# An earlier transpose of the dt rows, and another order in each MLP's last pair, in a one-core decoder step

## The chip, the cores and the metric

The kernel runs on one core of a Trainium2 chip. The time is that of the device for one execution, in microseconds (us). Below, PE is the tensor engine (matmul), DVE the vector engine, ACT the scalar engine, POOL the GpSimd engine and SP the engine that issues most transfers. "L367" is line 367 of the kernel before.

## What is computed

One step of a two-layer decoder trunk over 544 tokens: a prompt of 512, and 8 sequences of 4 tokens each with states of their own. The width is 1024, everything is float32.

```python
x = LN(alpha*x + ab_mixer(x));   x = LN(alpha*x + mlp(x))     # layer 0: mLSTM and GLA heads
x = LN(alpha*x + ssd_mixer(x));  x = LN(alpha*x + mlp(x))     # layer 1: Mamba-2 SSD
mlp(x) = square(relu(x @ w1)) @ w2                            # 1024 -> 4096 -> 1024
```

The SSD mixer needs, for each of 32 heads and each token, a step size and its running sums:

```python
dt = softplus(dtr + dt_bias);  a = dt * -exp(a_log)
cs = cumsum(a)                             # within a chunk
w  = exp(cs[t] - cs[s]) * dt[s]            # causal weights inside a chunk
wL = exp(cs[last] - cs) * dt               # weights of the chunk's final state
```

## The kernel before

Everything is held feature-major: features on the 128 partitions, tokens along the free dimension, in two halves of 272 tokens (`HALVES`). A float32 product is made of three products of a faster format: each operand is split into a high part (a cast on ACT, L166, L202, L286) and a low part (a subtraction on DVE, L167, L203, L287), and `hi*hi + hi*lo + lo*hi` accumulates in one PSUM bank. `dense` (L367) does this for one 128-column block of weights and one half of the tokens: 24 products for a depth of 1024. `WeightStream` loads the blocks in the order of use and splits them some blocks ahead.

**The order of the work.** PE's instructions run in the order in which the program writes them. The other engines' queues are ordered by the framework, which plans ahead of time by priority and by when it expects an instruction's inputs. Work beside the dense products is written as Python generators in lanes. `tick` is called ahead of every dense product; each lane counts its own ticks down and, at zero, writes its next piece. The counts stand in the table `W`. So a number in `W` says after how many dense products a piece stands in PE's queue.

**The SSD stage.** The first dense block of the stage gives `dt` before its softplus. `dt_rows` computes from it, on DVE and ACT, a tile `rows` with 32 partitions each of the running sums `cs`, of `dt` and of `dw` (the weights `wL`; its last operation is L1483). `rows` is one of two buffers that share the tag `E`. Then the generator `dt_cols` waits `W["dt"]` ticks from its launch, and transposes `rows` with five PE products into two PSUM banks, `rt` (L1489, L1490). Out of each bank it copies `cols` (L1493) and the negated `ncs` (L1494), and out of the second also `csp` (L1495). Then it says `dt` is ready. The generator `group(0)` in the lane "ssd" has waited for that: it transposes `Bf` into two banks (L1554, L1557), then in `scores` the tokens of the group into `xt` (L1578), multiplies `Cf` by `Bf` (`cb`, L1580), and goes on with `state` (L1614, L1617) and `outputs` (`yp`, L1639), with a fixed count of ticks between. Groups 1 to 3 follow in the same lane. All these small results take their PSUM bank in turn from four (`pm`). Meanwhile the convolution of the dense blocks runs on ACT (L1531, L1536) and DVE (`acc`, L1533; L1538, L1539).

**The MLP.** Hidden blocks 6 to 31 are made in pairs (`pair`) by a scheme of seven quarter products in place of eight. A quarter is 12 products (L563). The seven go into four banks `pa`, `pb`, `pc`, `pe`; three of the banks are used twice: the first sum of a bank is read, and then a second quarter accumulates onto it (`first=False`). The reads are `z = pa` (ACT, L623), `z += pb` (L626), `c22 = z + pc` (L629), `c22 += pe` (L632), then, after the second use, `c21 = z + pc` (L636), relu of `pa` (L612) and `c12 = z + pe` (L643). `act` makes of each result relu, square, high part and low part. `c21` and `pa` are the first half of the tokens, `c22` and `c12` the second. Pair 30 is the last; right after it the last part of the second matrix ("last", blocks 24 to 31) runs the first half of the tokens first, then the second. It reads block 30 at the seventh and block 31 at the eighth of its eight steps of depth.

Of the kernel before, what the change touches and what calls it, by code (L numbers as in the profile page):

```python
# [13 lines left out]
ALU = mybir.AluOpType  # L14
# [17 lines left out]
HEAD, TAIL = 5, 7  # L32
HEADM = 6

W = dict(dec=12, gates=30, gr=8, sc=16, lev=14, v=24, kd=10, out=38, ss=40, end=12, c0=20, u=13, s=16, ml=12, mr=40, dt=238, sg=72, sx=14, sq=26, so=48, l0=12, l1=12, v0=74, v1=55, f0=16, f1=18, f2=4, ls=20, vs=47)
LEVELS = (64, 32, 16, 8, 4, 2, 1)


# [189 lines left out]
def trunk_kernel(ctx, tc, a, stages=("ab", "mlp0", "ssd", "mlp1")):  # L228
    nc = tc.nc
    V, S, G, TE = nc.vector, nc.scalar, nc.gpsimd, nc.tensor  # L230
# [192 lines left out]
    def layernorm(hf, i, pool, out=None):  # L423
# [4 lines left out]
        which = norms_done[0] - hf  # L428
        yield W["l0" if not hf else "ls" if i == 2 else "l1"]
        mu = pm("mu")  # L430
# [8 lines left out]
        V.tensor_tensor(q[:, 0], q[:, 0], q[:, 1], ALU.add)  # L439
        yield W["v0" if not hf else "vs" if i == 2 else "v1"]  # L440
        var = pm("var")
# [34 lines left out]
    def last_layernorm(i, pool, out):  # L476
# [6 lines left out]
        def less(mu, k, f):  # L483
            V.scalar_tensor_tensor(x[:, k:k + 2], mu[:, None, :n].broadcast_to([P, 2, n]), f, x[:, k:k + 2], ALU.mult, ALU.add)
        yield W["f0"]
        mu = pm("mu")
# [9 lines left out]
        for k in range(h, KT - 1):  # L496
# [4 lines left out]
            V.tensor_tensor(q[:, 0], q[:, 0], q[:, k], ALU.add)  # L501
        yield W["f1"]
        mu, var, rp = pm("mu"), pm("var"), pm("rp")
        TE.matmul(mu[:, :n], ones, s, start=True, stop=False)
        yield W["f2"]
        TE.matmul(var[:, :n], ones, q[:, 0], start=True, stop=False)
# [50 lines left out]
    def quarter(w, b, ps, first):  # L557

        n = 0
        for k in range(4):  # L560
            for wt, bt in ((w[0], b[0]), (w[0], b[1]), (w[1], b[0])):
                tick()
                last[0] = TE.matmul(ps, wt[:, k], bt[:, k], start=first and n == 0, stop=n == 11, skip_group_check=not first).ins  # L563
                n += 1

    def mlp(l, phase_, outer, xp, out):
# [9 lines left out]
        bt = {}  # L576
# [31 lines left out]
        def act(m, hf, x, r=None):  # L608
            c0, c1 = HALVES[hf]
            h = place(m)  # L610
            r = hr() if r is None else r
            S.activation(r, x, AF.Relu)  # L612
            S.activation(r, r, AF.Square)
            split(h[0][:, c0:c1], h[1][:, c0:c1], r)

        def pair(m):
            w = ws.next()
            pa, pb, pc, pe = (bank()[:, :TH] for _ in range(4))
            hp = tc.high_priority
            z, c22, c21, c12 = (hr() for _ in range(4))  # L620
            quarter(w["a11"], bt["b11"], pa, True)
            with hp():
                S.copy(z, pa)  # L623
            quarter(w["s2"], bt["t2"], pb, True)
            with hp():
                V.tensor_tensor(z, z, pb, ALU.add)  # L626
            quarter(w["s3"], bt["t3"], pc, True)
            with hp():
                V.tensor_tensor(c22, z, pc, ALU.add)  # L629
            quarter(w["s1"], bt["t1"], pe, True)  # L630
            with hp():
                V.tensor_tensor(c22, c22, pe, ALU.add)  # L632
                act(m + 1, 1, c22, c22)
            quarter(w["a22"], bt["t4"], pc, False)
            with hp():
                V.tensor_tensor(c21, z, pc, ALU.add)  # L636
                act(m + 1, 0, c21, c21)
            quarter(w["a12"], bt["b21"], pa, False)
            with hp():
                act(m, 0, pa)  # L640
            quarter(w["s4"], bt["b22"], pe, False)
            with hp():
                V.tensor_tensor(c12, z, pe, ALU.add)  # L643
                act(m, 1, c12, c12)
# [10 lines left out]
        for kind, m, *r in MLP:  # L655
# [6 lines left out]
            if kind == "last":  # L662
                own.close()
                ws.lend(outer.enter_context(tc.tile_pool(name="hlx" + phase_, bufs=HLX, reuse_waits="tile")), phase_, HLX)
                end = None if out is None else lambda: last_layernorm(2 * l + 1, xp, out)
# [6 lines left out]
            for bs in blocks:  # L672
                w = ws.next()
# [720 lines left out]
    def ssd(pool, ypool, dram, right, ahead, consts):  # L1394
# [15 lines left out]
        cols = pool.tile([P, 5, 64], F32, name="scols", bufs=1)  # L1410
# [3 lines left out]
        dec = pool.tile([P, 32, 4], F32, name="dec", bufs=1)  # L1414
# [70 lines left out]
        def dt_cols():  # L1485
            yield W["dt"]
            p1, p2 = pm("rt"), pm("rt2")
            for b in range(4):
                TE.transpose(p1[:, b * 96:(b + 1) * 96], rows[:96, b * P:(b + 1) * P], ident[:96, :96])  # L1489
            TE.transpose(p2[:NS, :96], rows[:96, NP:], ident[:96, :96])  # L1490
            for o, b, q in ((slice(0, P), slice(0, 4), p1[:, :384].rearrange("p (b c) -> p b c", b=4)),
                            (slice(0, NS), slice(4, 5), p2[:NS, None, :96])):
                V.tensor_copy(cols[o, b], q[:, :, 32:])  # L1493
                V.tensor_scalar(ncs[o, b], q[:, :, :32], -1.0, None, ALU.mult)  # L1494
            V.tensor_copy(csp, p2[:NS, :32])  # L1495
            for r in (64, 96):
                S.activation(ecs[r:r + NS], ncs[:NS, 4], AF.Exp, scale=-1.0)
            ready.add("dt")
# [43 lines left out]
        Y, sqs, gates, tanh = [None] * 4, {}, {}, [None]  # L1542
# [327 lines left out]
    while n < len(stages):  # L1870
        st = stages[n]
        src = spill
        with ExitStack() as stk:
            if st == "ssd":
# [5 lines left out]
                with tc.tile_pool(name="ssd", bufs=1, reuse_waits="tile") as pool:  # L1880
# [4 lines left out]
                    with tc.manual_schedule(engines={mybir.EngineType.PE}):  # L1885
                        out = ssd(pool, ypool, dram, right, ahead, consts)
# [172 lines left out]
```

## Time and profile before

| what | us |
|---|---|
| median of three runs (1491.34 to 1493.38) | 1491.72 |
| the profiled execution | 1491.97 |
| its span, first to last instruction | 1490.2 |
| PE busy in it | 1468.6 |
| DVE busy | 1097.4 |
| ACT busy | 792.8 |

A row of the timeline gives the start, the duration, the engine, the line, the operation, what it writes and reads, and in brackets how long the engine stood idle ahead of it and what ended that. In the list of waits stand who waited for whom, and then the sum in us, the number of times and the longest. A product's row (0.29 us) is longer than its distance to the next one, since products overlap inside the engine.

### The profile page before, as it was taken

How to read it: one execution, taken by the hardware profiler on the slowest of the kernel's cores; microseconds unless marked ns; L12 is line 12 of the kernel's file. 1: busy time of each engine (PE TensorE's matmuls, PEld its weight loads, DVE VectorE, ACT ScalarE, POOL GpSimd, SP SyncE). 2: the span in 40 equal slices, each digit the busy share in tenths (PEclk: the TensorE clock that was granted, in tenths of full speed). 3: DMA queues.
4: the chain of work that ended last, by engine and by line, in shares of the span. 5: the costliest groups of instructions: out<-in, count | busy, mean ns of one | idle time of the engine just before them, and what ended most of it. 6: DMA issues, size and time to landing. Idle time of an engine off the chain costs nothing.

```text
span 1490.2 us, 29251 instructions
## 1 busy us (share of the span) xinstructions
PE 1468.6 (99%) x11637; PEld 1421.1 (95%) x11637; DVE 1097.4 (74%) x2073; ACT 792.8 (53%) x1746; POOL 190.8 (13%) x223
## 2 busy tenths in 40 slices
PE   9999999999999999999999999999999999999997
PEld 8999999999999999999888789899999999999996
DVE  4956576886776766678999988777588677676656
ACT  5645556473543453547886676555257355444333
POOL 0511231100000000010234342420010000000000
PEclk9999999999999999999999999999999999999999
DMA  6322325223332322525567866364222333233121
GB/s 225 97 71 58 117 60 167 73 69 98 100 92 94 97 88 71 156 98 161 136 185 228 255 182 209 100 211 138 72 75 71 99 97 99 86 100 100 57 86 60
DMA packets 94705, 172.90 MB, mean 116 GB/s; under 512 B 15960, under 2 KB 50392, under 8 KB 94312
## 3 DMA queue, kind: packets, MB, share of 16 engines
q1 hardware_dynamic: 61992, 140.86, 30.8%
q10 hardware_dynamic: 29216, 17.19, 4.5%
q0 software_dynamic: 3360, 12.98, 2.3%
q8 instruction: 91, 1.49, 0.4%
q14 instruction: 46, 0.38, 0.1%
HBM read 153.88 MB, written 17.13 MB: 115 GB/s over the span
## 4 chain that ended last, share of the span: by engine, by line
PE 43%; DVE 4%; DMA 2%; ACT 1%; issue 1%; POOL 0%; DVEq 0%; ACTq 0%; POOLq 0%
PE psd L367 30%; PE psd L563 9%; DMA E<-d_cs 2%; PE yp L1639 1%; PE it L1686 1%; DVE acc L1533 1%; DVE wlo L167 1%; PE sp L1617 1%; PE sps L1693 1%; DVE h0n L1699 0%; PE ip L1614 0%; ACT E L1599 0%; PE xt L1578 0%; POOL E L1593 0%; DVE xf L525 0%
## 5 line engine op out<-in xcount | busy, mean ns | idle before, releaser
L367 PE MATMUL psd<-xh,whi 128*128 128x272 f32 x1504 | 445.8, 296 | 0.1
L367 PE MATMUL psd<-xh,wlo 128*128 128x272 f32 x1504 | 439.9, 293 | 0.7 <-DVE wlo L167 0.7
L367 PE MATMUL psd<-xl,whi 128*128 128x272 f32 x1504 | 438.1, 291 | 1.8 <-DVE xl L451 1.3
L367 PE MATMUL psd<-hh,whi 128*128 128x272 f32 x1024 | 296.4, 289 | 0.7 <-ACT hh L286 0.7
L367 PE MATMUL psd<-hlo,whi 128*128 128x272 f32 x1024 | 295.9, 289 | 0.2
L367 PE MATMUL psd<-hh,wlo 128*128 128x272 f32 x1024 | 295.8, 289 | 0.0
L367 PEld LDWEIGHTS psd<-xl,whi 128*128 128x128 f32 x1504 | 284.1, 189 | 8.0 <-issue 4.2
L367 PEld LDWEIGHTS psd<-xh,whi 128*128 128x128 f32 x1504 | 283.5, 188 | 7.4 <-issue 5.1
L367 PEld LDWEIGHTS psd<-xh,wlo 128*128 128x128 f32 x1504 | 283.4, 188 | 4.9 <-issue 2.8
L167 DVE TENSOR_TENSOR wlo<-wraw,whi 128x1024 fp32r<-128x1024 f32 (+2 forms) x173 | 208.8, 1209 | 61.6 <-ACT whi L166 60.9
L166 ACT CAST whi<-wraw 128x1024 fp32r<-128x1024 f32 (+2 forms) x173 | 174.2, 1011 | 132.4 <-PE psd L367 114.8
L367 PEld LDWEIGHTS psd<-hh,whi 128*128 128x128 f32 x1024 | 193.1, 189 | 1.3 <-ACT hh L286 1.2
L367 PEld LDWEIGHTS psd<-hlo,whi 128*128 128x128 f32 x1024 | 193.0, 188 | 0.8 <-DVE hlo L287 0.6
L367 PEld LDWEIGHTS psd<-hh,wlo 128*128 128x128 f32 x1024 | 193.1, 189 | 0.1
L401 DVE TENSOR_TENSOR xf<-xf,psd 128x272 f32<-128x272 f32 x208 | 88.3, 434 | 75.9 <-PE psd L367 75.4
L563 PE MATMUL psd<-xh,wlo 128*128 128x272 f32 x416 | 120.1, 289 | 0.0
L563 PE MATMUL psd<-xh,whi 128*128 128x272 f32 x416 | 119.9, 288 | 0.0
L563 PE MATMUL psd<-xl,whi 128*128 128x272 f32 x416 | 119.8, 288 | 0.0
L202 ACT CAST whi<-wsum 128x1024 fp32r<-128x1024 f32 x52 | 54.3, 1044 | 111.0 <-PE psd L563 70.2
L202 ACT CAST whi<-wraw 128x1024 fp32r<-128x1024 f32 (+1 forms) x52 | 43.4, 834 | 95.3 <-PE psd L367 84.2
L203 DVE TENSOR_TENSOR wlo<-wsum,whi 128x1024 fp32r<-128x1024 f32 x52 | 63.7, 1224 | 23.2 <-ACT whi L202 23.2
L563 PEld LDWEIGHTS psd<-xl,whi 128*128 128x128 f32 x416 | 78.5, 189 | 0.0
(474 smaller groups left out, 2778.2 us busy)
## 6 DMA issues: line engine op xcount, KB each, us to landing
wraw<-mlp_w SPq DMA_DIRECT2D x80, 512.0 KB, 3.6
wraw<-ssd_in SPq DMA_DIRECT2D x40, 512.0 KB, 4.0
wraw<-mlp_w SPq DMA_DIRECT2D x64, 256.0 KB, 3.1
wraw<-ab_in SPq DMA_DIRECT2D x24, 512.0 KB, 3.6
h<-h SPq DMA_DIRECT2D x32, 256.0 KB, 4.9
h0n<-h0n SPq DMA_DIRECT2D x16, 512.0 KB, 5.7
E<-d_cs ACTq DMA_DIRECT2D x16, 512.0 KB, 4.5
s_h<-h0n POOLq DMA_DIRECT2D x16, 512.0 KB, 4.1
```

Of the source, the lines that this page charges most:

```text
L166: nc.scalar.copy(hi[:, r], w[:, r])
L167: nc.vector.tensor_tensor(lo[:, r], w[:, r], hi[:, r].bitcast(F32), ALU.subtract)
L202: self.cut[0] = nc.scalar.copy(hi, x).ins
L203: self.cut[1] = nc.vector.tensor_tensor(lo, x, hi.bitcast(F32), ALU.subtract).ins
L367: last[0] = TE.matmul(ps[:, :TH], wt[:, k, :], rt, start=i == 0, stop=i == n - 1).ins
L401: V.tensor_tensor(x, x, ps, ALU.add)
L563: last[0] = TE.matmul(ps, wt[:, k], bt[:, k], start=first and n == 0, stop=n == 11, skip_group_check=not first).ins
L1533: V.scalar_tensor_tensor(acc[:, :n], ci[:, w:w + n], cw[:, m, w:w + 1], acc[:, :n], ALU.mult, ALU.add)
L1617: TE.matmul(sp, Bt[:, b], xw, start=True, stop=True)
L1639: TE.matmul(ypv[64 * e:64 * e + 64, j], z[:, 64 * r:64 * r + 64], E[:, r], start=True, stop=True)
L1686: TE.matmul(it[64 + NS * k:64 + NS * k + NS], Cm[:, NS * (q + k):NS * (q + k) + NS], h0[k], start=q == 0, stop=q == NB - 2)
L1693: TE.matmul(sp[:, 256 * j:256 * j + 256], Xs[:, m * P:(m + 1) * P], Bm.rearrange("p k n -> p (k n)"), start=True, stop=True)
```

## The change

`W["dt"]` goes from 238 to 224 ticks. The two copies of `cols` go from DVE to ACT. In pair 30 of each MLP the two quarters that end the first half of the tokens come ahead of s1; the other pairs stay as they are.

```diff
-W = dict(..., dt=238, ...)
+W = dict(..., dt=224, ...)
...
-            quarter(w["s1"], bt["t1"], pe, True)
-            with hp():
-                V.tensor_tensor(c22, c22, pe, ALU.add)
-                act(m + 1, 1, c22, c22)
-            quarter(w["a22"], bt["t4"], pc, False)
-            with hp():
-                V.tensor_tensor(c21, z, pc, ALU.add)
-                act(m + 1, 0, c21, c21)
-            quarter(w["a12"], bt["b21"], pa, False)
-            with hp():
-                act(m, 0, pa)
+
+            def second():
+                quarter(w["s1"], bt["t1"], pe, True)
+                with hp():
+                    V.tensor_tensor(c22, c22, pe, ALU.add)
+                    act(m + 1, 1, c22, c22)
+
+            def first():
+                quarter(w["a22"], bt["t4"], pc, False)
+                with hp():
+                    V.tensor_tensor(c21, z, pc, ALU.add)
+                    act(m + 1, 0, c21, c21)
+                quarter(w["a12"], bt["b21"], pa, False)
+                with hp():
+                    act(m, 0, pa)
+
+            for half in (first, second) if m == 30 else (second, first):
+                half()
             quarter(w["s4"], bt["b22"], pe, False)
...
-                V.tensor_copy(cols[o, b], q[:, :, 32:])
+                S.copy(cols[o, b], q[:, :, 32:])
                 V.tensor_scalar(ncs[o, b], q[:, :, :32], -1.0, None, ALU.mult)
```

More of the change, by code (lines that the diff above doesn't have):

```diff
@@ L33 @@
 HEADM = 6
-W = dict(dec=12, gates=30, gr=8, sc=16, lev=14, v=24, kd=10, out=38, ss=40, end=12, c0=20, u=13, s=16, ml=12, mr=40, dt=238, sg=72, sx=14, sq=26, so=48, l0=12, l1=12, v0=74, v1=55, f0=16, f1=18, f2=4, ls=20, vs=47)
+W = dict(dec=12, gates=30, gr=8, sc=16, lev=14, v=24, kd=10, out=38, ss=40, end=12, c0=20, u=13, s=16, ml=12, mr=40, dt=224, sg=72, sx=14, sq=26, so=48, l0=12, l1=12, v0=74, v1=55, f0=16, f1=18, f2=4, ls=20, vs=47)
 LEVELS = (64, 32, 16, 8, 4, 2, 1)
```

## The prediction, made before the changed kernel ran

> **What bounds the kernel now.** I read the page's head first, then the list of waits of the tensor engine, then the rows around each wait that the diff touches.
>
> ```profile
> span 1490.2 us, 29251 instructions
> PE 1468.6 (99%) x11637; PEld 1421.1 (95%) x11637; DVE 1097.4 (74%) x2073; ACT 792.8 (53%) x1746; POOL 190.8 (13%) x223
> ...
> PEclk9999999999999999999999999999999999999999
> ```
>
> The matmul queue is the bound: PE is busy for 99% of the span at a full clock. The change neither adds nor drops a product, so the time can move only by what PE waits.
>
> ```profile
> PE xt L1578 <- DVE ncs L1494: 2.2, 1, 2.2
> PE yp L1639 <- DVE ec L1615: 2.1, 3, 0.8
> ...
> PE psd L367 <- ACT hh L286: 0.7, 2, 0.4
> ```
>
> The first wait is the one that the dt half of the change meets: PE stands 2.2 us because a read of the transposed rows is late. The third stands once at the end of each MLP. The second lies later in the SSD stage.
>
> The pace of the products comes from the chain of waits:
>
> ```profile
> 1164.40 10.51 PE psd L563 x84
> ```
>
> That is one whole pair: 84 products in 10.51 us, so 0.125 us each and 1.50 us for a quarter of 12 (the 0.29 us that a row shows is the product's own depth).
>
> **The change, part one: the order inside pair 30.** Quarters now run a11, s2, s3, a22, a12, s1, s4; before, s1 stood after s3. What it can remove, in the first MLP (from 612 us) and the second:
>
> ```profile
> 612.67 0.29 PE L367 MATMUL psd<-hh,wlo 128*128 128x272 f32 x1
> 613.33 0.39 PE L367 MATMUL psd<-hh,whi 128*128 128x272 f32 x1 [0.37 <-ACT hh L286]
> 613.80 0.39 PE L367 MATMUL psd<-hlo,whi 128*128 128x272 f32 x1
> 614.03 0.28 PE L367 MATMUL psd<-hh,wlo 128*128 128x272 f32 x1
> ...
> 1430.34 0.39 PE L367 MATMUL psd<-hh,whi 128*128 128x272 f32 x1 [0.36 <-ACT hh L286]
> ```
>
> Start to start these take 0.66, 0.47 and 0.23 us instead of 0.125 each: 0.99 us lost per MLP, because the first half of hidden block 30 comes late. The new order finishes that half 3 us (two quarters) earlier, so all of it should go: -0.99 each.
>
> What it adds is a wait on PSUM. Quarter a22 accumulates into `pc`, the bank that s3 has just filled, and `c22 = z + pc` must have read it first. Before, s1 (into `pe`) ran in between and hid that read. In the same way s4 accumulates into `pe` straight after s1, while `c22 += pe` is still to read it; before, a22 and a12 stood between. The trace of before shows the length of this read:
>
> ```profile
> 604.40 0.29 PE L563 MATMUL psd<-t3h,wlo 128*128 128x272 f32 x1
> 604.52 0.29 PE L563 MATMUL psd<-t1h,whi 128*128 128x272 f32 x1
> ```
> ```profile
> 604.73 0.44 DVE L629 TENSOR_TENSOR hr<-hr,psd 128x272 f32<-128x272 f32 x1 [0.65 <-PE psd L563]
> 606.22 0.44 DVE L632 TENSOR_TENSOR hr<-hr,psd 128x272 f32<-128x272 f32 x1 [1.06 <-PE psd L563]
> ```
>
> The last product of s3 starts at 604.40; the read runs 604.73 to 605.17, with DVE idle before it. A waiting product starts about 0.05 us after its release (613.33 follows the cast that ends at 613.28, below), so a22 starts at 605.22 instead of 604.52: 0.70 us. After a stop the next product takes 0.23 us instead of 0.125 (613.80 to 614.03): 0.10 more. So 0.80 us for pc, and the same for pe, since L632 is also released by PE and also takes 0.44. Bounds for one: 0.70, if the restart costs nothing, and 1.24, if DVE is in a low-part subtraction of 0.44 us when the read is due. I take 0.80, because both rows show DVE idle ahead of the read. Per MLP 1.60 - 0.99 = +0.61; **two MLPs +1.2 us** (+0.8 to +3.0).
>
> What else moves there, at nothing:
>
> ```profile
> 607.50 2.93 ACT L166 CAST whi<-wraw 128x1024 fp32r<-128x1024 f32 x3
> ...
> 612.87 0.41 ACT L286 CAST hh<-hr 128x272 fp32r<-128x272 f32 x1
> ```
> ```profile
> 597.73 0.69 DVE L203 TENSOR_TENSOR wlo<-wraw,whi 128x512 fp32r<-128x512 f32 x1
> ...
> 613.31 0.44 DVE L287 TENSOR_TENSOR hlo<-hr,hh 128x272 fp32r<-128x272 f32 x1 [0.20 <-ACT hh L286]
> ```
>
> The a22 weights, split last, are ready at 598.4, 6 us ahead of their new place. Three weight casts of the last phase occupy ACT for 2.93 us; if their room is t1's, they start up to 3 us later, and are covered, since the last phase first uses up two blocks that are already split. If they stay early, they stand before the activations of block 30: a12 ends at 608.5, and 2.93 for the casts, two rounds of three activations and a subtraction give about 614.3, while the product that needs it would stand at 614.4. Without that cover a wait of up to 0.4 us returns.
>
> **The change, part two: the dt rows.** `W["dt"]` falls from 238 to 224, so five transposes come 14 x 0.125 = 1.75 us earlier, and the whole "ssd" lane with them; two copies of the result (`cols`) go from DVE to ACT. No product vanishes; 14 products come after the wait instead of before it.
>
> ```profile
> 721.68 0.49 PE L1489 MATMUL rt<-scon,rows 96*128 96x96 f32 x4
> ...
> 722.53 0.27 PE L1557 MATMUL Bts<-scon,Bf 128*32 128x128 f32 x1
> 725.02 0.63 PE L1578 MATMUL xt<-scon,Y 128*128 128x128 f32 x4 [2.21 <-DVE ncs L1494]
> 725.49 0.39 PE L1580 MATMUL cb<-Cf,Bf 128*128 128x128 f32 x2
> ```
> ```profile
> 718.73 0.72 DVE L1483 TENSOR_TENSOR rows<-rows 32x544 f32<-32x544 f32 x1
> 719.48 0.81 DVE L1533 SCALAR_TENSOR_TENSOR acc<-ci,sprm,acc 128x568 f32<-128x568 f32 x1
> 720.21 1.22 DVE L167 TENSOR_TENSOR wlo<-wraw,whi 128x1024 fp32r<-128x1024 f32 x1
> 721.34 0.81 DVE L1533 SCALAR_TENSOR_TENSOR acc<-ci,sprm,acc 128x568 f32<-128x568 f32 x1
> 722.06 1.58 DVE L1538 SCALAR_TENSOR_TENSOR Cf<-Cf,acc 128x512 f32<-128x512 f32 x1
> 723.56 0.18 DVE L1539 SCALAR_TENSOR_TENSOR Cf<-Cf,acc 128x32 f32<-128x32 f32 x1
> 723.67 0.41 DVE L1493 COPY scols<-rt 128x256 f32<-128x256 f32 x1
> ...
> 724.60 0.28 DVE L1494 TENSOR_SCALAR ncs<-rt 128x128 f32<-128x128 f32 x1
> ...
> 725.13 0.17 DVE L1495 COPY csp<-rt 32x32 f32<-32x32 f32 x1
> ```
>
> The fifth use of the banks, `xt`, takes the bank of the first transposes and waits until `ncs` has read it at 724.88. The transposes were done by 722.3; DVE was late because older work of the convolution stood ahead. Nothing in the change shortens that older work, and it leaves no gap from 718.73 on. So coming 1.75 us sooner helps only if `ncs` may go ahead of it. I take the nearest place: `ncs` gets the slot of the copy that leaves, 723.67 to 723.95, and `xt` follows 0.14 us after, as before, at 724.09. With the 14 products still owed, 724.09 + 1.75 - 725.02 = **+0.8 us**. The next, `cb`, needs the last read of the second bank, `csp`. Without the small copy and the order's tail that ends between 724.5 and 724.9; cb, 0.47 after xt, could start at 724.56. So 0 to 0.4 more, and I take 0.2. Bounds of the whole: -0.8, if `ncs` runs at 722.06 ahead of Cf (722.34 + 0.14 + 1.75 - 725.02), and +2.2 (third rival). The rows are complete at 719.45 and would be wanted at 719.9: 0.4 us of cover, the price if it is gone about one acc, 0.8 us less 0.4.
>
> ```profile
> 719.39 0.37 ACT L1520 COPY ci<-psd 128x272 f32<-128x272 f32 x1
> 722.18 0.63 ACT L1536 ACTIVATE Y<-acc 128x512 f32<-128x512 f32 x1 [2.42 <-DVE acc L1533]
> ...
> 723.84 0.86 ACT L1531 ACTIVATE acc<-ci,sprm 128x568 f32<-128x568 f32 x1 [0.90 <-DVE Cf L1539]
> ```
>
> ```profile
> 718.74 0.35 ACTq L1570 DMA_DIRECT2D E<-d_cs  x1
> ...
> 723.92 0.37 ACTq L1570 DMA_DIRECT2D E<-d_cs  x1
> ```
>
> Of the lane's transfers the first are issued ahead of the transposes. `rows` holds one of the two `E` buffers, so the one at 723.92 comes only once the transposes have read it, and may now come up to 1.75 us sooner. I cost that at nothing too: the list of waits has no PE wait on such a transfer.
>
> The ACT copy costs about 0.36 us (0.37 for the 272 columns of L1520) and fits into ACT's idle 2.42 us before 722.18. That is why I cost it at nothing.
>
> **Sum:** 1.2 + 0.8 + 0.2 = +2.2 us on the profiled execution's 1491.97, so 1494.2; that execution stands 0.25 above the median of the runs, 1491.72, so for a median I say **1493.9**. About 0.2% (3 us) is what a measurement of this kernel can tell from no change; the forecast lies inside it.
>
> **The rivals.** *First, faster: the change does all it is meant to.* No read of pc or pe holds PE (-0.99 twice), and the xt wait goes wholly (-2.2): 1491.7 - 4.2 = 1487.5. For it stand the named waits; against it the two reads that nothing covers any more. 6%.
>
> *Second: `ncs` overtakes the convolution.* -0.8 + 1.2 = +0.4: 1492.1. For it: the transposes are ready in DVE's order some instructions sooner; against: conv work, older in program order, was always served first. 17%.
>
> *Third, slower: the ACT copy comes late and holds `ncs`.* Two engines read one bank, and the end of the kernel shows how that goes:
>
> ```profile
> 1480.03 0.69 ACT L525 ACTIVATE lnq<-mu 128x272 f32<-128x272 f32 x2 [0.35 <-PE mu L509]
> ```
> ```profile
> 1480.74 0.72 DVE L525 SCALAR_TENSOR_TENSOR xf<-mu,xf 128x544 f32<-128x544 f32 x1 [1.53 <-ACT lnq L525]
> ```
>
> `mu` was ready at 1480.03, but DVE's read starts at 1480.74, 0.02 us after ACT's two reads of it. So `ncs` cannot pass the copy on ACT. If that copy is placed behind the acc of 723.84 (ends 724.70), it ends near 725.02, `ncs` at 725.30, xt starts at 725.44: 725.44 + 1.75 - 725.02 = +2.2, with the MLPs +3.4, so 1495.1. It decides from the point where the copy misses ACT's idle time before 722.18. 20%. [...]
>
> *Fourth, slower: the three yp waits (2.1 us) double,* since the lane meets a DVE that is just as full 1.75 us of products earlier: 1496.0. For it: they end on DVE's `ec`; against: the lane's own reads move earlier too. 12%.
>
> **How the numbers follow.** The forecast has 45%, with its own range 1492.9 to 1495.2. Slower by over 0.2% (above 1494.7): a fifth of the forecast, three quarters of the third and most of the fourth: 0.09 + 0.15 + 0.10 = 0.34. Faster by over 0.2% (below 1488.7): the first rival and a trace of the second: 0.07. The rest, 0.59, is no change. The range leaves out the first rival below and ends above at the fourth's 1496.0 with the pe bound of 1.24 in both MLPs: 1490.2 to 1496.8.
>
> **What would show it.** Right: a PE row on L563 with a gap of some 0.4 us ahead of it (the 0.29 depth hides the rest), released by DVE L629, and one by L632, in each MLP; no wait on hh L286 at the start of the last phase; the xt wait on `ncs` longer than 2.2 us, not shorter. Wrong: no such PE rows, or an `xt` that waits less than 0.5 us, or yp waits whose sum leaves 1.5 to 2.7 us.

## The result, and the profile after

| | before | after |
|---|---|---|
| median of the runs that were taken side by side | 1492.25 (6 runs) | 1498.57 (6 runs) |
| ratio, 95% interval | | 1.004 (1.003 to 1.005) |
| profiled execution | 1491.97 | 1497.5 |
| its span | 1490.2 | 1495.8 |

The change makes the kernel 6.0 us slower, where +2.2 was predicted. That is outside the predicted range (1490.2 to 1496.8). From the page of the changed kernel:

```profile
PE 1470.8 (98%) x11637; PEld 1422.6 (95%) x11637; DVE 1094.2 (73%) x2071; ACT 795.4 (53%) x1748; POOL 184.7 (12%) x223
```

The products are the same 11637; the 5.6 us of span are waits, and, as will be seen, a little clock. The list of PE's waits in the changed kernel (who waited <- for whom: us in total, times, longest). Lines behind the MLP are 7 higher than before.

```profile
PE sps L1700 <- DVE Xs L1672: 2.4, 1, 2.4
PE psd L367 <- DVE hlo L287: 1.8, 2, 0.9
PE cb L1587 <- DVE Cf L1546: 1.6, 2, 1.0
PE xt L1585 <- ACT Bt L1562: 1.5, 1, 1.5
...
PE psd L563 <- DVE hr L629: 1.2, 2, 0.6
...
PE psd L563 <- DVE hr L634: 1.1, 2, 0.5
PE cb L1587 <- DVE Cf L1545: 0.8, 1, 0.8
```

Gone are the waits on `hh`, on `ncs` and all `yp` waits on `ec`. New are the two on `hr` that the prediction named, and others that it did not: on `hlo`, on `Cf`, and at `xt` on `Bt`. The wait on `Xs` was 0.4 us before.

**Where the time went, by stage.** Four rows of PE, the first product of the last group of pair products and the first of the layernorm behind the MLP; before, then after:

```profile
589.47 0.29 PE L563 MATMUL psd<-xh,whi 128*128 128x272 f32 x1
...
640.18 0.39 PE L431 MATMUL mu<-lns,ones 128*128 128x272 f32 x1
```
```profile
589.41 0.29 PE L563 MATMUL psd<-xh,whi 128*128 128x272 f32 x1
...
642.06 0.39 PE L431 MATMUL mu<-lns,ones 128*128 128x272 f32 x1
```

50.71 us against 52.65: the first MLP loses 1.94. Between the same two rows the second MLP loses 1.88. From that row of the layernorm to the first `nv` product at the SSD stage's end (925.83 before, 929.51 after) it is 285.65 against 287.45, a loss of 1.80. With 0.06 gained ahead of all this that makes 1.94 + 1.88 + 1.80 - 0.06 = 5.56, the whole difference.

**In the MLP.** PE's rows of the changed kernel around the two bank reads, and in the last phase:

```profile
604.34 0.29 PE L563 MATMUL psd<-t3h,wlo 128*128 128x272 f32 x1
605.25 0.36 PE L563 MATMUL psd<-xh,whi 128*128 128x272 f32 x1 [0.62 <-DVE hr L629]
605.45 0.29 PE L563 MATMUL psd<-xl,whi 128*128 128x272 f32 x1
...
609.71 0.29 PE L563 MATMUL psd<-t1h,wlo 128*128 128x272 f32 x1
610.53 0.39 PE L563 MATMUL psd<-xh,whi 128*128 128x272 f32 x1 [0.53 <-DVE hr L634]
610.76 0.29 PE L563 MATMUL psd<-xl,whi 128*128 128x272 f32 x1
...
617.42 0.39 PE L367 MATMUL psd<-hh,whi 128*128 128x272 f32 x1
618.72 0.39 PE L367 MATMUL psd<-hlo,whi 128*128 128x272 f32 x1 [0.91 <-DVE hlo L287]
618.95 0.29 PE L367 MATMUL psd<-hh,wlo 128*128 128x272 f32 x1
```

Start to start, less 0.125 for each product: 0.91 and 0.20 lose 0.86 at the first bank, 0.82 and 0.23 lose 0.80 at the second, 1.30 and 0.23 lose 1.28 at the third place. Sum 2.94, less the 0.99 of the wait on `hh` that is gone: 1.95. The measured 1.94 is thus accounted for. The third place is the second half of hidden block 30 in the last phase. ACT's rows and DVE's there:

```profile
609.60 0.42 ACT L286 CAST hh<-hr 128x272 fp32r<-128x272 f32 x1
610.04 2.95 ACT L166 CAST whi<-wraw 128x1024 fp32r<-128x1024 f32 x3
...
614.59 0.43 ACT L613 ACTIVATE hr<-hr 128x272 f32<-128x272 f32 x1
616.00 1.05 ACT L166 CAST whi<-wraw 128x1024 fp32r<-128x1024 f32 x1 [0.98 <-DMA wraw<-mlp_w]
616.96 0.41 ACT L286 CAST hh<-hr 128x272 fp32r<-128x272 f32 x1
```
```profile
617.09 1.23 DVE L167 TENSOR_TENSOR wlo<-wraw,whi 128x1024 fp32r<-128x1024 f32 x1 [1.30 <-ACT whi L166]
618.23 0.44 DVE L287 TENSOR_TENSOR hlo<-hr,hh 128x272 fp32r<-128x272 f32 x1
```

The square (L613) is done at 615.02, and its cast could follow. But the next instruction in ACT's queue is the cast of a weight block whose transfer has not landed. ACT stands 0.98 us, casts the weights, and only then the hidden block, at 616.96. DVE has its own weight instruction first in the same way. The row of three casts at 610.04 stood at 607.50 before, and SP issues the next three transfers of weights from 612.37 on and not from 609.82, 2.55 us later. The cast of block 30's first half (609.60) now stands ahead of the three casts; before, it stood behind them, at 612.87.

**In the SSD stage.** The start of the first group: PE, then DVE, then ACT.

```profile
721.79 0.49 PE L1496 MATMUL rt<-scon,rows 96*128 96x96 f32 x4
...
724.43 0.66 PE L1585 MATMUL xt<-scon,Y 128*128 128x128 f32 x4 [1.51 <-ACT Bt L1562]
725.66 0.46 PE L1587 MATMUL cb<-Cf,Bf 128*128 128x128 f32 x2 [0.57 <-DVE Cf L1546]
```
```profile
725.54 0.37 DVE L1501 TENSOR_SCALAR ncs<-rt 128x128 f32<-128x128 f32 x2
```
```profile
722.32 0.47 ACT L1500 COPY scols<-rt 128x256 f32<-128x256 f32 x2 [0.69 <-PE rt L1496]
723.38 0.37 ACTq L1577 DMA_DIRECT2D E<-d_cs  x1
723.79 0.59 ACT L1562 COPY Bt<-Btp 128x512 f32<-128x512 f32 x1 [1.00 <-DVE wlo L167]
```

`xt` no longer waits for `ncs`, which reads `rt` a full 1.1 us after `xt` has started. It waits for the copy of `Bt`, so it must have been given the bank of the `Bf` transposes; why, no run shows. That copy stands in ACT's queue behind the issue of a transfer, which starts at 723.38 though ACT's last work had ended at 722.79. The row of the copy names DVE's `wlo`, which ended at 723.30, as what ended ACT's wait.

Then the place of the first sample products, DVE of the changed kernel:

```profile
766.33 1.83 DVE L1540 SCALAR_TENSOR_TENSOR acc<-ci,sprm,acc 128x568 f32<-128x568 f32 x1
...
769.62 1.47 DVE L1672 TENSOR_TENSOR Xs<-xw,Xs 32x512 fp32r<-32x512 f32 x1
```

`Xs` needs only 1.47 us of DVE, but rows of the convolution stand ahead of it from 766.33 on, and PE stops for the 2.4 us of the list. Behind this stop the granted clock is 0.55 and then 0.52. Windows of the changed kernel (start:end, length, busy us of PE, PEld, DVE, ACT and POOL, granted clock, DMA share, GB/s):

```profile
771.20:772.00 0.80, 0.77 (x4) 0.80 (x5) 0.80 (x2) 0.80 (x3) 0.00 (x0) 0.55 0.02 3
772.00:774.80 2.80, 2.80 (x14) 2.80 (x14) 2.80 (x9) 2.80 (x10) 0.10 (x1) 0.52 0.26 32
```

From the end of the stop for 3.6 us PE runs at about half its clock: 14 products in 2.8 us, where the pace of 0.125 us makes 22.

**The SSD stage cut at its `xt` products.** Each of its groups writes five sets of `xt` at fixed places, so the starts of these sets cut the stage into pieces with the same content in both kernels. Only the 14 products are moved: they are missing in the first row of the table and come back in its last row but one, with one more that the pieces up to 815.61 have lost. As an example, here are the rows that begin and end the piece with the first sample products, before and after:

```profile
758.95 0.28 PE L1578 MATMUL xt<-scon,Y 128*32 128x128 f32 x1
...
778.60 0.27 PE L1578 MATMUL xt<-scon,Y 128*128 128x128 f32 x1
```
```profile
758.49 0.38 PE L1585 MATMUL xt<-scon,Y 128*32 128x128 f32 x2
...
781.26 0.38 PE L1585 MATMUL xt<-scon,Y 128*128 128x128 f32 x2
```

| piece (start before) | before | after | difference |
|---|---|---|---|
| layernorm to `rt` | 81.50 | 79.73 | -1.77 (14 products fewer) |
| `rt` to the first `xt` | 3.34 | 2.64 | -0.70 |
| first `xt` (725.02) | 5.48 | 6.28 | +0.80 |
| three pieces up to 758.95 | 28.45 | 27.78 | -0.67 |
| first sample products (758.95) | 19.65 | 22.77 | **+3.12** |
| four pieces up to 815.61 | 37.01 | 36.39 | -0.62 |
| second sample products (815.61) | 21.00 | 18.97 | **-2.03** |
| four pieces up to 874.90 | 38.28 | 39.04 | +0.76 |
| third (874.90) | 46.40 | 48.30 | +1.90 (15 products more) |
| last group, 921.30 to `nv` | 4.53 | 5.55 | **+1.02** |

The sum is +1.81. So the waits on `yp` did go, but a longer one came at `Xs`, with a slow clock behind it, and one at the last group's `cb`, on `Cf`.

### The profile page after: what moved, and what is told of

The parts are those of the page before. It is cut to its first block, busy times and chain, and to the rows that moved or that the text cites. A ratio compares the mean times of both kernels' runs of the same rounds, so it can differ in the third digit from the quotient of the medians.

```text
span 1495.8 us, 29256 instructions
## 1 busy us (share of the span) xinstructions
PE 1470.8 (98%) x11637; PEld 1422.6 (95%) x11637; DVE 1094.2 (73%) x2071; ACT 795.4 (53%) x1748; POOL 184.7 (12%) x223
## 5 line engine op out<-in xcount | busy, mean ns | idle before, releaser
L367 PEld LDWEIGHTS psd<-xh,whi 128*128 128x128 f32 x1504 | 283.7, 189 | 8.7 <-issue 6.4
L367 PEld LDWEIGHTS psd<-xl,whi 128*128 128x128 f32 x1504 | 284.0, 189 | 6.9 <-issue 3.0
L563 PEld LDWEIGHTS psd<-xh,whi 128*128 128x128 f32 x416 | 78.2, 188 | 3.1 <-issue 1.6
```

Source lines behind the costliest of these rows:

```text
L367: last[0] = TE.matmul(ps[:, :TH], wt[:, k, :], rt, start=i == 0, stop=i == n - 1).ins
```

## The experiments

Times below are medians, beside those of the kernel before that was run along with them. Where a difference is given in us with a ratio, it is (ratio - 1) times before's median.

### One part of the change alone

The MLP's new order, with the dt edit left out:

```diff
-W = dict(..., dt=224, ...)
+W = dict(..., dt=238, ...)
...
-                S.copy(cols[o, b], q[:, :, 32:])
+                V.tensor_copy(cols[o, b], q[:, :, 32:])
```

> Only the new order in pair 30; W["dt"] is 238 again and DVE makes both copies of cols. Theory (ledger of the two traces): each MLP pays 0.79 us at the a22 quarter, 0.69 at s4, 0.1 after each, and 1.2 us where the second half's low part of block 30 is late (618.7 us in the changed kernel), and saves 0.99: +1.9 per MLP, +3.7 us in all, with the SSD stage as before. Rival (my prediction's sum): the late low part is one execution's accident and goes with the shifted SSD stage; then +1.2 us and no wait on hlo.

Measured: 1497.27 against 1492.81, ratio 1.0025 (1.0016 to 1.0033), +3.7 us. In its list of waits the three of the changed kernel's MLP are all there, on `hlo` and twice on `hr`, with the same sums. The MLPs cost 1.94 and 1.99 in this profile, the SSD stage 0.35 less than before. So the order alone makes the MLP's loss, and it is the larger part.

The dt part alone, as the fragment above has it but with the old order, in three forms: both edits, the ticks alone, the copy alone.

```diff
-W = dict(..., dt=238, ...)
+W = dict(..., dt=224, ...)      # first and second form
...
-                V.tensor_copy(cols[o, b], q[:, :, 32:])
+                S.copy(cols[o, b], q[:, :, 32:])      # first and third form
```

> Only the dt part: W["dt"] 224 and the cols copies on ACT; pair 30 in its old order. Theory: the PE waits of the SSD stage sum to the same 6.7 us, but two of them melt into one of 2.4 us at sps, after which the granted clock is about 0.5 for some 3.5 us: +1.8 us, nearly all of it the clock. Rival: the waits themselves grow (over 8 us in sum) at a full clock, and that gives the +1.8.

> W["dt"] 224 alone, the cols copies stay on DVE. Theory: it is the lane that comes 14 products earlier that runs into the saturated DVE at sps: as e2, +1.8 us, with the sps wait over 2 us and the slow clock after it. Rival: the copies on ACT re-order ACT's and DVE's queues and make the sps wait; then this one is within 0.5 us of before.

> Only the cols copies on ACT, W["dt"] stays 238. Theory: xt waits 1 us less (ncs takes the slot of the copy that leaves DVE, or xt gets another bank), and the waits that hang on DVE later take most of it back: -0.7 to +0.2 us, clock full. Rival (the copies are the cause of the changed kernel's SSD loss): +1.8 us with the long sps wait.

Measured: both 1494.42, ratio 1.0008 (1.0000 to 1.0017); the ticks alone 1495.68, 1.0015 (1.0007 to 1.0024); the copy alone 1494.06, 1.0006 (0.9995 to 1.0017); before 1492.81. The intervals overlap, so the two edits can't be ranked; no form is shown to gain. With 1.2 us for both, the halves add: 3.7 + 1.2 = 4.9, against 6.0 (4.5 to 7.5) for the whole change. In their profiles `xt` waits 1.9 us for `ncs` if only the copy moves, and 1.3 us for `Bt` if only the ticks do; a wait on `E` at a `yp`, 1.8 us with the copy alone and 2.4 us with the ticks alone, stands in these two where `Xs` stands with both. Neither edit alone makes the stop at `Xs` (0.8 and 0.7 us there), so neither the mechanism that was expected of the ticks alone nor the rival for the copy alone is borne out.

### The casts at the head of ACT's queue

Both kernels of the next pair hold the casts of the last phase's weights in ACT's order behind the last cast of hidden block 30. One has the new order, one the old; neither has the dt part.

```diff
-            for i in self.cut:
+            for i in (*self.cut, self.hold):
                 if i is not None:
                     after.enter_context(self.tc.issue_after(i))
...
-                act(m, 1, c12, c12)
+                done = act(m, 1, c12, c12)
+            if m == 30:
+                ws.hold = done
```

> The new order of pair 30 (no dt part), and every weight cast of the last phase is issued on ACT only behind the high part of the second half of block 30 (L286 of c12). Theory: in the changed kernel that high part stands behind a cast which itself waits for its transfer (ACT idle 615.0 to 616.0), and this alone makes the 1.2 us wait on hlo; so that wait goes and the two reads of pc and pe stay: the rest per MLP is 1.7 - 0.99 = +0.7, in all +1.3 us against before, some 2.5 less than the order alone (+4.4). Rival: the second half is late because its quarters end 1.6 us later; then the wait on hlo stays at 0.5 us or more and the kernel stays over +3.

> The kernel before with its old order, and the same hold on the weight casts of the last phase. Theory: the 0.99 us wait on hh at the start of the last phase comes from three casts (2.93 us on ACT) ahead of block 30's activations, not from the order of the quarters; so it goes without a new wait: -2.0 us. Rival: the order of the quarters makes it; then it stays at 0.7 us or more per MLP, 0.0 us. A third way: the last phase's weights now come late; then a wait on wlo stands at blocks 2 to 5 and the kernel is slower.

Measured: new order 1494.07 against 1493.36, ratio 1.0004 (0.9995 to 1.0013), +0.6 us. Old order 1490.31, ratio 0.9979 (0.9970 to 0.9988), -3.1 us (-4.5 to -1.8), faster than both kernels of this case. ACT's rows in the new order:

```profile
613.96 0.42 ACT L287 CAST hh<-hr 128x272 fp32r<-128x272 f32 x1
614.29 2.94 ACT L167 CAST whi<-wraw 128x1024 fp32r<-128x1024 f32 x3
```

The three casts now come last, in the old order as well, and no wait on `hh` or `hlo` is left in either. PE's row in the new order and in the old, first product of the pairs' last group and first of the layernorm:

```profile
589.64 0.29 PE L564 MATMUL psd<-xh,whi 128*128 128x272 f32 x1
...
641.02 0.39 PE L432 MATMUL mu<-lns,ones 128*128 128x272 f32 x1
```
```profile
591.01 0.29 PE L564 MATMUL psd<-xh,whi 128*128 128x272 f32 x1
...
640.73 0.39 PE L432 MATMUL mu<-lns,ones 128*128 128x272 f32 x1
```

51.38 and 49.72 against 50.71 before: +0.67 and -0.99. Two things follow. The third wait of the new order was made by casts ahead on ACT: it goes when they do, and what is left, 0.67, is the two bank reads less the old wait (1.66 - 0.99). And the wait on `hh` that the change was able to remove had the same cause: the old order loses it, all 0.99 us, without any change of the quarters. The two MLPs of its trace give 2.0 of the 3.1 us measured; the rest lies within the interval.

The bank reads were then hidden in another order, a12 ahead of s1 and a22 behind it, with the hold and without the dt part (the fragment is against the changed kernel, whose two functions become three):

```diff
-            for half in (first, second) if m == 30 else (second, first):
-                half()
+            for part in (a12, s1, a22) if m == 30 else (s1, a22, a12):
+                part()
```

> The dt part as before; the last pair in the order a11, s2, s3, a12, s1, a22, s4, so that one quarter lies between each read of a PSUM bank and the next product into that bank, and the last phase's casts held as in the run before. Theory: the two bank reads are what is left of the cost of the changed order once the casts are held (0.65 us per MLP); with a quarter between them they are hidden, and this kernel comes out like the old order with the hold, about 3 us under before, ratio 0.998, with no wait on hr and none on hh or hlo in the pair. Rival: the 0.65 us is owed to block 31's second half coming later, as in the changed kernel; then there is a wait on block 31 at the start of its products, and no gain over the changed order with the hold (1494 where before is 1493).

The new order in it, told against before, is a11, s2, s3, a12, s1, a22, s4, so at least one quarter of 1.50 us lies over each read. Measured: 1490.43 against 1492.70, ratio 0.9987 (0.9979 to 0.9996), -1.9 us. Its MLP takes 49.73, as the old order with the hold (49.72), and no wait on `hr` is listed. So 0.67 was the price of the uncovered reads. The order itself brings nothing once the casts are held. ("As before" in the expectation means as in the kernel before: this kernel has no dt part.)

### Does the half clock, or the stop ahead of it, make the dt part's loss?

First with products of no use, 18 in the code, at the places where PE stops: ahead of `xt` in the first group and ahead of the first `sps` with the dt part alone, and only ahead of `xt` in the kernel before. They change no output. The fragment is the first place.

```diff
+            if g == 0:
+                f = psm.tile([P, 512], F32, tag="k", name="fill", bufs=1)
+                for _ in range(18):
+                    TE.matmul(f[:, :P], ones, ones, start=True, stop=True)
```

> The dt part alone (as e2), with 18 extra 128-column products of ones that nobody reads ahead of the waits of xt (group 0) and of the first sps, so that PE works where it stood still. Theory: the stops themselves are hidden work, so the extra products cost little, and the slow clock after them (3.6 us near 772, 2.5 us near 726) goes: granted clock 1.0 there, 1 to 2 us less than e2 (+1.6). Rival: the clock falls whatever PE does there, or the extra products push the lane: no gain over e2, or slower.

> The kernel before with the same 18 extra products ahead of the xt wait alone. Theory: in some executions of the kernel before too the 2.2 us stop at xt is followed by a slow clock, which makes the spread of its times (1490.4 to 1497.2); then the upper times go and the median falls by 0.5 to 1 us. Rival: the spread is from elsewhere; median and spread stay as before, within 0.5 us, or the extra products add up to 1 us.

Measured: 1507.21, ratio 1.0092 (1.0079 to 1.0106), and 1495.74, ratio 1.0017 (1.0008 to 1.0026), before 1493.36. Both miss. In the second the filling is the reason:

```profile
722.77 4.18 PE L1562 MATMUL fill<-ones 128*128 128x128 f32 x36
```

The trace has two instructions for each of the 18, so 36 ran, 4.18 us to cover a stop of 2.2: `xt` starts at 726.79 and not at 725.02. In the first kernel they set the lane back by more than that (waits of 3.5 us on `xw` and 2.9 on `Cf`). Neither speaks for or against the clock.

Next, the subtractions for `Xs` and the smaller `Bs` were put ahead of DVE's other work, by priority: with the dt part alone, with the old order and hold, and with the f1 order and hold.

```diff
-                V.tensor_tensor(lo, s_, o[0:32].bitcast(F32), ALU.subtract)
+                with tc.high_priority():
+                    V.tensor_tensor(lo, s_, o[0:32].bitcast(F32), ALU.subtract)
```

> The dt part alone (rows transposed at 224, the copy on ScalarE), and beside it the subtractions of the small blocks' low parts (Bs and Xs, each with 0.4 to 1.5 us of VectorE) put ahead of whatever else VectorE has. Theory: the dt part alone costs about 1.6 us because the wait it removes comes back at the sample products, 2.4 us on the low part of Xs, which stands behind two rows of the convolution and one of Bf; a stop of that length also lets the clock fall. With the low part ahead this wait falls under 0.7 us, and the time comes 1.6 to 2.5 us below that of the dt part alone: 0 to 1 us faster than before, 1492 to 1493.5 where before is 1493. Rival 1: the loss of the dt part is the other stop, at xt, which moves on to the copy of Bt and keeps 1.5 us and the slow clock behind it; then nothing changes here, 1.6 us slower than before. Rival 2: VectorE is full there, and what is put behind the low part (Bf, the convolution) makes TensorE wait at cb or psd instead; then the Xs wait goes and a wait of the same size shows on another tile.

> The old order of the quarters with the last phase's weight casts held on ScalarE behind the hidden block's last cast (3.05 us faster than before, measured), the dt part, and the low parts of Bs and Xs ahead of VectorE's other work. Theory: the pieces lie in different stages and add: -3 from the hold, 0 to -1 from the dt part with Xs ahead, so 1489 to 1490.5 where before is 1493, a ratio of 0.9973 to 0.998. Rival: the dt part loses 1.6 us whatever Xs does; then 1491.5, a ratio of 0.999.

> The last run's order and hold together with the dt part and the low parts of Bs and Xs ahead. Theory: -3 from the hold, 0 to -1 from the dt part, nothing from the order itself: 1489 to 1490.5 where before is 1493, equal to the old order with hold, dt part and Xs ahead. Rival: the order loses or gains in the MLP's last phase, which then shows as a difference of 0.6 us or more per MLP between the two.

Measured, against 1492.70: 1494.62, ratio 1.0016 (1.0008 to 1.0024); 1491.99, 0.9996 (0.9987 to 1.0004); 1491.35, 0.9991 (0.9982 to 1.0000). The wait on `Xs` stays at 2.4 us in all three: the priority did not move the subtraction past the convolution, so what was to be tested was not. They serve as three more measurements of the dt part, with this edit still in them: +2.4 us alone; +2.5 on top of the old order with the hold (-0.6 against -3.1); +0.6 on top of the f1 order (-1.3 against -1.9, intervals that overlap). With the 1.2 of the first run, the dt part costs 0.6 to 2.5 us in four comparisons.

And they price the clock. The same piece, with the same stop of 2.4 us: the dt part alone with the priority, first row the stop, then the rows that cut the piece, then the window behind the stop:

```profile
770.76 0.72 PE L1694 MATMUL sps<-Bm,Xs 96*128 96x256 f32 x4 [2.44 <-DVE Xs L1666]
```
```profile
758.01 0.60 PE L1578 MATMUL xt<-scon,Y 128*32 128x128 f32 x4
...
779.27 0.60 PE L1578 MATMUL xt<-scon,Y 128*128 128x128 f32 x4
```
```profile
771.60:774.40 2.80, 2.80 (x25) 2.80 (x24) 2.80 (x9) 2.80 (x10) 0.10 (x1) 1.00 0.52 119
```

21.26 us, at full clock. In the changed kernel, in the dt part alone, and in the two other kernels with the priority the clock fell (0.50 to 0.55), and the piece takes 22.77, 22.72, 22.72 and 22.77. So the slow clock is worth 1.5 us, and the stop with the rest of the piece 21.26 - 19.65 = 1.6, which is its 2.4 us less the 0.8 of a `yp` wait in the same piece of before.

The falls are not the dt part's own, though. The stop at the first `xt` is 2.21 or 2.22 us in all five profiles with no dt edit and the usual place of the sample products. The clock stayed at 1.00 around it in three of them (before, the order alone, the order with the hold) and fell in two (the old order with the hold, the f1 order; the mean granted clock of each of the two profiles is 0.996, of before 0.998), where that piece takes 6.85 and 6.79 us and not 5.48 to 5.88. From the layernorm to `nv`, before and the order alone have no fall and the other three one each; the five with both dt edits (the changed kernel, the dt part alone, and the three with the priority) have 1, 2, 1, 2 and 1 (mean granted clock 0.996, 0.995, 0.997, 0.995 and 0.996). That is 0.8 more on the mean. At 1.5 us each, an estimate from the pair above, it makes 1.2 us.

Then the subtraction was moved to GpSimd, with PE's order left as it is: with the dt part alone, and with the f1 order and hold too.

```diff
-                V.tensor_tensor(lo, s_, o[0:32].bitcast(F32), ALU.subtract)
+                (V if d == 1 else G).tensor_tensor(lo, s_, o[0:32].bitcast(F32), ALU.subtract)
```

> The dt part alone, with the subtraction for the low part of Xs on GpSimd in place of VectorE; TensorE's order is that of the dt part alone. Theory: the stop at the first sample products (2.4 us) and the half clock behind it (2.8 us, worth 1.4) are what turns the dt part from a gain to a loss. GpSimd is free at about 767.9 and takes some 1.3 us, so the stop falls to 0.5 to 1 us, the clock stays, that segment takes 20 us and not 22.8, and the kernel comes 2 to 3.4 us below the dt part alone: 0.5 to 1.8 us faster than before, ratio 0.9988 to 0.9997. Rival: what is lost here is gained back later through the slack that VectorE has (the later segments take what the first ones lose), so the end moves by less than 0.7 us though the stop is gone; then the ratio stays at 1.001 and cb's wait for Cf in the last group (1.0 us) and xt's for Bt are the loss.

> The last pair in the order a11, s2, s3, a12, s1, a22, s4 with the casts held, the dt part, and the subtraction for the low part of Xs on GpSimd. Theory: about 2.5 us below before from the MLPs and 0.5 to 1.8 us from the SSD stage: 1488.5 to 1490 where before is 1493, ratio 0.997 to 0.998. Rival: as for the dt part alone, the loss of the SSD stage stays and the ratio is 0.999 to 1.

Measured, against 1493.09: 1498.36, ratio 1.0040 (1.0027 to 1.0052), and 1494.79, 1.0008 (0.9999 to 1.0018). The subtraction takes 3.07 us on GpSimd, where DVE took 1.47 in the changed kernel and 1.68 in the kernel before:

```profile
769.68 3.07 POOL L1665 TENSOR_TENSOR Xs<-xw,Xs 32x512 fp32r<-32x512 f32 x1
```

The expectation had 1.3, an estimate; in the kernel before, GpSimd's operations on 128x512 elements take 1.28 us on the mean at L1027 and 2.12 at L1644. At 3.07, PE still stops 1.9 us at `sps`, and new waits of 2.4 us (`cb` on `Cf`) and 1.5 us (`sp`) come up behind. In the second of the two the clock stayed full behind this stop and the piece takes 20.76 us, where the same kernel with the priority took 22.77; yet the pieces behind it lose more than that. What the dt part would cost without the stop can't be read from either.

Last, the first sample products of each group were put 20 products later in PE's order: with the dt part alone; with the f1 order, the hold and the dt part; and with the f1 order and hold without the dt part.

```diff
-                yield W["sq"]
+                yield W["sq"] + (20 if q == 0 else 0)
```

> The dt part alone, and the first two sample blocks of each group 20 products (2.5 us) later in TensorE's order. Theory: the wait of 2.4 us for the low part of Xs is covered by products and the half clock behind it goes; the segment from the fifth xt to the sixth takes 19.5 to 20.5 us instead of 22.7, and the time comes 2 to 3 us below the dt part alone, 0.4 to 1.4 us under before, ratio 0.999 to 0.9997. Rival: the segment shortens, but VectorE, which has the same work to do, makes the later segments longer by the same (waits at cb, sp or yp on Cf, h0n or E grow by 2 to 3 us in sum), and the ratio stays at 1.001 to 1.0015.

> The last pair in the order a11, s2, s3, a12, s1, a22, s4 with the casts held, the dt part, and the first sample blocks 20 products later. Theory: 2 to 3 us under before from the MLPs and 0.4 to 1.4 from the SSD stage: ratio 0.9970 to 0.9983. Rival: 0.9985 to 0.9995, the SSD stage as slow as with the dt part alone.

> The same without the dt part: the control. If the later sample blocks gain by themselves, apart from the dt part, this kernel is faster than the order with the hold alone (ratio 0.9987 there); theory says it is the same within 0.0005, since there the wait for Xs was 0.4 us or less; rival: it gains or loses 1 us or more, and the effect in the two others has to be read against that.

Measured, against 1493.50: 1504.20, ratio 1.0060 (1.0045 to 1.0075); 1503.45, 1.0057 (1.0043 to 1.0072); 1493.92, 1.0003 (0.9995 to 1.0012). The wait on `Xs` is gone and the piece takes 17.31 us and not 22.7, with 8 small products fewer in it. But the next piece, which has them, takes 12.17 and not 6.93, and more is lost later: PE's longest wait in the first of the three is 3.7 us, of a `cb` on `Cf`.

That is the rival of that expectation, and beyond it. Even the control loses 2.4 us by the same shift (1.0003 against the 0.9987 of the f1 order with the hold, each to its own before). A likely reason is in the window of the whole stage in the kernel before.

```profile
725.00:925.00 200.00, 195.55 (x1549) 171.00 (x1550) 183.40 (x319) 141.05 (x417) 73.37 (x80) 1.00 0.69 207
```

DVE is busy for 183.4 of these 200 us, though for 74% only of the span. With so little slack, a wait of PE that is covered at one place can come back at another as soon as DVE's order suffers. It fits these runs, but no run took work off DVE to test it.

## Why the prediction was wrong, step by step

- **The bank reads: right.** 0.80 was taken for each; 0.86 and 0.80 were measured, and both rows were named ahead (L629; the second read's line is 634 in the changed kernel). The gaps in the rows are 0.62 and 0.53 us, where some 0.4 was expected.
- **The wait on `hh`: right in size, wrong in its reason.** 0.99 us went in each MLP. It was to go because the half would end two quarters, 3 us, earlier. But only s1 moved behind that half: one quarter, 1.50 us, less the 0.8 lost at the bank read. The last product of a12 starts at 608.21 and not at 608.92. What went was the cause that was not asked for: the three casts ahead of it on ACT now stand behind, so its cast comes 3.27 us earlier (609.60, not 612.87). The run with the old order and the hold shows that moving the casts is enough.
- **"What else moves there, at nothing": wrong, and the largest miss.** That step followed only the first half of block 30 past the three casts, and allowed up to 0.4 us for it if they stayed early. They came 2.5 us later, as its other branch had it, and that branch was costed at nothing. The second half was not followed. It meets the cast behind those three, which waits for its transfer at the head of ACT's queue, and then DVE's: 1.28 us per MLP, 2.6 in all. The prediction's sum for the MLPs was +1.2; it came to 3.8. With the casts held the MLP comes out at +0.67, beside the predicted +0.61.
- **The start of the SSD lane: mechanism wrong, the sum near.** `xt` was to wait for `ncs` (+0.8), and `cb` for `csp` (+0.2). `ncs` came where it was assumed, right behind `Cf`: 725.54 in the changed kernel is 723.66 in the time of the kernel before, since the first MLP sets everything back by 1.94 - 0.06 = 1.88. But it no longer decided: `xt` got another bank and waited for the copy of `Bt`: -0.70. `cb` then waited for `Cf`, its own operand, and comes 1.23 us behind `xt` and not 0.47: +0.76. Together 0.1, where 1.0 was predicted. That the issue of `E`, costed at nothing, stands ahead of the `Bt` copy is read from the rows; no run took it away.
- **The later waits: a term of the sum that was missing.** They were left as they were, and the fourth rival doubled them. They vanished instead (-2.1; in the other profiles with no dt edit and the usual place of the sample products their sum is 1.1 to 3.2, so it is not a steady term), and other products now meet DVE late: `sps` on `Xs` (2.4 us, where it was 0.4) and the last `cb` on `Cf`. That last piece takes 7.22 or 7.23 us, first `xt` to the next, in the five profiles with both dt edits that were counted above, 7.20 with the ticks alone and 6.45 with the copy alone, and 6.19 in the five with no dt edit. So its 1.03 us comes with the ticks. The clock behind the `Xs` stop adds 1.5 in this execution. The SSD stage comes to +1.8, where +1.0 was predicted.
- **The rivals.** The first did not come, since the bank reads held PE. The second did not: `ncs` stayed behind `Cf`. The third did not either: ACT's copies ran at 722.32, early. That `ncs` can't pass such a copy was the author's inference from one pair of rows, and no run tested it. The fourth is the opposite of what happened to `yp`. By the prediction's own signs the dt part was wrong: the sum of `yp` waits is outside 1.5 to 2.7 us, and `xt` waits 1.5 us for `Bt`, where over 2.2 us for `ncs` was to show it right.
- **The range** ended at 1496.8, since both bounds for the MLP's unknown concerned the bank reads; a third wait was in none of them. Its lower end, 1490.2, is worked out from no row.

**What stays open.** The stage's loss is located (the pieces in bold), and its clock is priced; why `xt` changes its bank, and why DVE takes the convolution ahead of `Xs`, is not shown. Whether the dt part would gain if `Xs` came in time is not settled: the priority did not move it, GpSimd took 3.07 us for it, and the later products upset DVE's order. Single profiles of this stage also differ among themselves. From the layernorm to `nv` it takes 285.3 to 286.0 us in four profiles without the dt part and 288.2 in a fifth, and 286.9 to 288.8 in five with it. The means differ by 1.6. With the estimate of 1.2 for the falls of the clock, only some 0.4 us of that is left for the waits themselves, and five profiles a side are too few to say whether the dt part makes falls more frequent.

## What to carry to other kernels

When a result is to come earlier, follow every half of it through each engine's queue up to its last reader, and look at what stands directly ahead of it there: here a weight cast that stood 0.98 us for its transfer came ahead of a cast that could have run from 615.02, and that one started at 616.96. Before work is reordered around a wait, find out whether the producer is late or only queued late; here one ordering constraint on ACT brought 0.99 us per MLP, all that the new order of products could, with no new wait in the MLP. And in a stage where a second engine is busy for 92% of the time, a wait that is removed is no gain until the end of the stage has been seen to move. Before a difference between two single traces is put down to a change, count in how many places the clock fell in each (none to two in the SSD stage of the ten profiles here).

## What the runs showed of the hardware

The granted clock was 0.50 behind two stops of PE of 1.37 and 0.71 us, and 1.00 behind one of 3.27 us. In the kernel with the dt part alone and the priority, PE's stops at the first `xt` and `cb` are 1.37 and 0.71 us; the window behind them is the first row. In the kernel with the dt part alone and later sample products one `yp` stops PE for 3.27 us; its row and a window behind it follow (the 1 us between them is at 1.00 too).

```profile
724.90:726.40 1.50, 1.50 (x8) 1.50 (x8) 1.47 (x5) 1.48 (x7) 1.16 (x3) 0.50 0.90 282
```
```profile
803.96 0.80 PE L1639 MATMUL yp<-E,z 128*64 128x32 f32 x18 [3.27 <-ACT cb L1592]
```
```profile
805.00:807.00 2.00, 2.00 (x22) 1.83 (x19) 2.00 (x4) 1.05 (x3) 1.78 (x3) 1.00 0.26 35
```

At `Xs` a stop of 2.4 us had 1.00 behind it in the kernel with the dt part alone and the priority, and 0.50 to 0.55 in the four others. Behind the stop of 2.2 us at the first `xt` the clock stayed at 1.00 in three profiles and fell in two. So in these profiles the length of a stop alone does not tell whether the clock falls.

On GpSimd a subtraction of 32x512 float32 took 3.07 us, against 1.47 on DVE in the changed kernel and 1.68 in the kernel before.
